# First top-k selections of six tiles moved into the joint query's loop, and index conversions on ScalarE

## The chip, the cores and the metric

The kernel runs on one core of a Trainium2 chip. The core has a matrix engine (TensorE, PE in the profile, with its weight loads as PEld), a vector engine (VectorE, DVE), an activation engine (ScalarE, ACT), a general engine (GpSimd, POOL) and an engine that only issues DMAs here (SyncE, SP). ScalarE and GpSimd issue DMAs too, in line with their other work. Each engine runs its instructions in a fixed order and waits on semaphores for the others.

The metric is the device time of one launch in microseconds, lower is better; the time before is the median of three runs.

## The reference

The kernel computes one layer of a hybrid decoder for 1024 prompt tokens and 8 x 8 sample tokens: a retention and an RWKV-7 mixer, a PEER expert layer, and a gated per-layer embedding. The change lies in the PEER part:

```python
q = (xb @ wq).reshape(PEER_BLOCK, PEER_HEADS, 2, PEER_DKEY // 2)
s = jnp.einsum('phcd,hcnd->phcn', q, keys).astype(jnp.float32)
sv, si = lax.top_k(s, PEER_TOPK)
cand = sv[:, :, 0, :, None] + sv[:, :, 1, None, :]
cv, ci = lax.top_k(cand.reshape(PEER_BLOCK, PEER_HEADS, PEER_TOPK * PEER_TOPK), PEER_TOPK)
e = (jnp.take_along_axis(si[:, :, 0], ci // PEER_TOPK, axis=-1) * PEER_NKEYS
     + jnp.take_along_axis(si[:, :, 1], ci % PEER_TOPK, axis=-1))
gsm = jax.nn.softmax(cv, axis=-1)
hval = jnp.einsum('pd,phkd->phk', xb, u_tab[e])
act = (jax.nn.gelu(hval.astype(jnp.float32), approximate=False) * gsm).astype(xb.dtype)
return jnp.einsum('phk,phkd->pd', act, v_tab[e])
```

For each token and each of 8 heads, the token's query is scored against two sets of 128 keys. The 16 best of each set are kept (the *first* selection, 16 of them per token: 8 heads x 2 halves). Their sums are candidates; the 16 best of these (the *second* selection) give 16 experts a head, 128 a token, out of 16384. Each expert is a row of `u_tab` and a row of `v_tab`, 1024 numbers each.

## The kernel before

The tokens form nine tiles, 0 to 8, of 128 tokens (tile 8, the samples, has 64). Three groups are handled in different ways in the PEER part:

- Tiles 0, 1 and 8 (`E0`) have a query of their own (`early_query`, L1172) and *gather* their expert rows: `gather` (L1117) fetches, for one expert slot of all tokens at a time, a row per token by an indirect DMA that GpSimd issues (L1127). VectorE multiplies it with the tokens and sums (L1141), once for each of 128 slots (64 for tile 8); then the same again for `v_tab`, where VectorE adds the weighted row to the accumulator (L1155).
- Tiles 2 and 3 (`G1`) share the joint query with the next group, then are gathered like the first.
- Tiles 4 to 7 (`G2`) are computed *densely*: hidden values of all 16384 experts by matmuls in 128 blocks (`hidden`, L1256), multiplied with a dense matrix of gates, and multiplied with `v_tab` (`dense`, L1285).

There is one accumulator for all gathers, so the five gathered tiles follow each other: 0, 1, 8, 2, 3.

The joint query, `c_query` (L1005), runs over 16 pairs of head and half. For each it loads the weights, splits them into a high part (ScalarE) and a low part (VectorE and GpSimd by turns, `split`, L295), multiplies both tile groups by them (three matmuls each for full precision), copies the result with ScalarE (L1023), multiplies with the keys (L1026) and copies the 128 scores a token with ScalarE into a tile `ss` (L1027). After every second pair the scores are stored to memory (`sd`, L1030).

`topk` (L1033) is run for each of these six tiles in the stage after the query. It loads the scores of all 16 pairs (L1038) and makes the first selections on VectorE: the eight largest (L1043), their places (L1044), their removal (L1045), the next eight (L1046) and their places (L1047). Then the places become floating-point numbers `sf` (L1050, L1051), candidates and their expert numbers are added up (L1058 to L1065, VectorE and GpSimd), the second selection is made (L1069 to L1073), its places are converted to `cf` (L1076) and looked up by a comparison with a row of numbers (L1082 to L1084), the softmax is formed (L1094 to L1099), and for the dense tiles the expert number is divided into its two halves (L1111 to L1115, `e12`).

`gates` (L1227) makes the dense gates of one tile: it transposes `e12` and the softmax on TensorE, copies the latter (L1234, `it`), and for every four tokens builds two one-hot matrices on VectorE (L1242), scales one of them on ScalarE (L1244), multiplies them on TensorE (L1247) and copies the product with ScalarE (L1248).

The stage after the query is written out in `build`: for each dense tile in turn its `topk` is interleaved with the `gates` of the tile before, followed by a fifth of the first 96 hidden blocks (`NPRE`); `topk` and `gather` of tile 2 stand behind the second such step, those of tile 3 behind the last. Then come the other 32 hidden blocks with the dense matmuls, and at last `ple` (L1373) with the final norm, which needs the accumulators of the gathered tiles.

The order of instructions on each engine isn't the written one. A planner in the framework simulates the program when it is built, with the written order as priority, and fixes the order on each engine by when things come ready in its simulation (`schedule_with_timeline_sim=True`). The rest of the early gathers is written behind the joint query (`run(query)`, then `run(early)`).

Of the kernel before, what the change touches and what calls it, by code (L numbers as in the profile page):

```python
# [8 lines left out]
F32 = mybir.dt.float32  # L9
# [3 lines left out]
U32 = mybir.dt.uint32  # L13
AF = mybir.ActivationFunctionType
OP = mybir.AluOpType
# [163 lines left out]
G1 = [2, 3]  # L179
# [11 lines left out]
G2 = [4, 5, 6, 7]  # L191
RSTART = 2
RRATE = 1
ERATE = 1
QB = 4
EB = 150
SIZE = {t: (64 if t == 8 else 128) for t in range(9)}


def spans(tiles):  # L200

    e = [sum(SIZE[t] for t in tiles[:i]) for i in range(len(tiles) + 1)]
    return dict(zip(tiles, e)), e[-1]
# [8 lines left out]
class K:  # L212
# [482 lines left out]
    def rw_mix(self, t):  # L695
# [282 lines left out]
        if t == 7:  # L978
            self.tail = self.ep0.tile([128, 512], F32, name="tail", tag="Wq", bufs=QB)
            nc.vector.tensor_tensor(self.tail, xf, p, op=OP.mult)  # L980
# [24 lines left out]
    def c_query(self, wp, da, parts):  # L1005

        nc, I = self.nc, self.I
        for hc in range(16):
            kT = wp.tile([128, 128], F32, name="keysT")
            nc.sync.dma_start(kT, I['keysT'][:, hc])  # L1010
            raw = da.tile([128, 8, 128], F32, name="wqr", tag="uraw", bufs=UB)
            nc.sync.dma_start(raw, I['wq'][hc])
            wh = da.tile([128, 8, 128], F32R, name="wqh", tag="uh", bufs=DW)
            wl = da.tile([128, 8, 128], F32R, name="wql", tag="ul", bufs=DW)
            self.split(wh, wl, raw, "g" if hc % 2 else "v")
            if hc % 2 == 0:
                st = [wp.tile([128, len(tiles), 2, 128], F32, name=f"ss{tiles[0]}", bufs=1) for tiles, _ in parts]
            for (tiles, x), s in zip(parts, st):
                off, n = spans(tiles)
                p = self.ps("pq", "b")  # L1020
                self.mm3(p[:, :n], lambda k: wh[:, k, :], lambda k: wl[:, k, :], lambda k: x[0][:, k], lambda k: x[1][:, k], 8)
                qT = wp.tile([128, n], F32, name=f"qT{tiles[0]}", bufs=1)
                nc.scalar.activation(qT, p[:, :n], AF.Copy)  # L1023
                p = self.ps("psc", "a")
                for i, t in enumerate(tiles):
                    nc.tensor.matmul(p[:SIZE[t], i * 128:i * 128 + 128], qT[:, off[t]:off[t] + SIZE[t]], kT, start=True, stop=True)  # L1026
                nc.scalar.activation(s[:, :, hc % 2], p[:, :len(tiles) * 128].rearrange("p (t k) -> p t k", k=128), AF.Copy)  # L1027
                if hc % 2:
                    for i, t in enumerate(tiles):
                        nc.scalar.dma_start(self.sd[t][:SIZE[t], hc - 1:hc + 1], s[:SIZE[t], i])  # L1030
            yield

    def topk(self, tp, t, s=None, tags={}, ce=None):  # L1033
        nc = self.nc
        n = SIZE[t]
        if s is None:
            w = tp.tile([128, 16, 128], F32, name="s", bufs=1)
            nc.sync.dma_start(w[:n], self.sd[t][:n])  # L1038
            s = [w[:, j] for j in range(16)]
        sv = tp.tile([128, 16, 16], F32, name="sv")  # L1040
        si = tp.tile([128, 16, 16], U32, name="si")
        for hc in range(16):
            nc.vector.max(sv[:n, hc, 0:8], s[hc][:n])  # L1043
            nc.vector.max_index(si[:n, hc, 0:8], sv[:n, hc, 0:8], s[hc][:n])  # L1044
            nc.vector.match_replace(s[hc][:n], sv[:n, hc, 0:8], s[hc][:n], -3.0e38)  # L1045
            nc.vector.max(sv[:n, hc, 8:16], s[hc][:n])  # L1046
            nc.vector.max_index(si[:n, hc, 8:16], sv[:n, hc, 8:16], s[hc][:n])  # L1047
            yield
        sf = tp.tile([128, 8, 2, 16], F32, name="sf")
        nc.vector.tensor_copy(sf[:n].rearrange("p h c k -> p (h c) k"), si[:n])  # L1050
        nc.vector.tensor_scalar(sf[:n, :, 0], sf[:n, :, 0], 128.0, None, op0=OP.mult)  # L1051
        svv = sv.rearrange("p (h c) k -> p h c k", c=2)
        cand, eid = ce or [tp.tile([128, 8, 50], F32, name=n) for n in ("cand", "eid")]
        for src, dst, eng in ((svv, cand, nc.vector), (sf, eid, nc.gpsimd)):
# [12 lines left out]
        ci = tp.tile([128, 8, 16], U32, name="ci")  # L1067
# [5 lines left out]
            nc.vector.max_index(ci[:n, h, 8:16], cv[:n, h, 8:16], cand[:n, h])  # L1073
            yield
        cf = tp.tile([128, 128], F32, name="cf")
        nc.vector.tensor_copy(cf[:n], ci[:n].rearrange("p h k -> p (h k)"))  # L1076
        ef = tp.tile([128, 128], F32, name="ef")
        io = self.c("iota")[:n, None, :50].to_broadcast([n, 16, 50])
        for h in range(8):
# [21 lines left out]
        if t == 8:  # L1101
            ei = tp.tile([128, 128], I32, name="ei", tag="ex")
            nc.vector.tensor_copy(ei[:n], ef[:n])
            for k in range(2):
                nc.scalar.dma_start(self.eid[t][64 * k:64 * k + 64], ei[:64, 64 * k:64 * k + 64])
                nc.scalar.dma_start(self.gsm[t][64 * k:64 * k + 64], gsm[:64, 64 * k:64 * k + 64])
        elif t not in G2:
            nc.vector.tensor_copy(self.eid[t][:n], ef[:n])
        else:
            ei = tp.tile([128, 128], I32, name="ei", tag="ex")  # L1110
            nc.vector.tensor_copy(ei[:n], ef[:n])  # L1111
            e1 = tp.tile([128, 2, 128], I32, name="e1")
            nc.vector.tensor_scalar(e1[:n, 0], ei[:n], 7, None, op0=OP.logical_shift_right)
            nc.vector.tensor_scalar(e1[:n, 1], ei[:n], 127, None, op0=OP.bitwise_and)
            nc.vector.tensor_copy(self.e12[t][:n], e1[:n])  # L1115

    def gather(self, gp, t, rows=("grow",), parts=1, acc=None):  # L1117

# [53 lines left out]
    def early_query(self, wp, t, wtag, wbufs, stags):  # L1172
# [31 lines left out]
        for j in range(2):  # L1204
            s.append(wp.tile([128, 8, 128], F32, name="es", tag=stags[j], bufs=QB if stags[j] == "Wq" else 1))
            nc.sync.dma_start(s[j][:n], self.sd[t][:n, 8 * j:8 * j + 8])
        yield
        ce = wp.tile([128, 2, 8, 50], F32, name="ce", tag="Wq", bufs=QB)
        yield from self.topk(wp, t, [s[j // 8][:, j % 8] for j in range(16)], dict(eq=dict(tag="xT")), (ce[:, 0], ce[:, 1]))
# [17 lines left out]
    def gates(self, wp, t):  # L1227
        nc = self.nc
        n, o = SIZE[t], self.off[t]
        p = self.ps("pit", "i").rearrange("p (a b) -> p a b", a=4)  # L1230
        for j, src in enumerate((self.e12[t][:n, 0], self.e12[t][:n, 1], self.gsm[t][:n])):
            nc.tensor.transpose(p[:, j, :n], src, self.c("ident")[:n, :n])
        it = wp.tile([128, 128], F32, name="it", bufs=2)
        nc.vector.tensor_copy(it[:, :n], p[:, 2, :n])  # L1234
        io = self.c("iota")[:, None, :].to_broadcast([128, 4, 128])
        for s in range(0, n, 64):
            last = (o + s) // 64 == self.ntok // 64 - 1
            st = self.stage[(o + s) // 64 % 2].tile([128, 128, 64], F32, name="wst", bufs=1)
            for b in range(0, 64, 4):
                oh = [wp.tile([128, 4, 128], F32, name=f"oh{j}", bufs=2) for j in range(2)]  # L1240
                for j in range(2):
                    nc.vector.tensor_tensor(oh[j], io, p[:, j, s + b:s + b + 4, None].to_broadcast([128, 4, 128]), op=OP.is_equal)  # L1242
                for j in range(4):
                    nc.scalar.activation(oh[0][:, j], oh[0][:, j], AF.Copy, scale=it[:, s + b + j:s + b + j + 1])  # L1244
                pw = self.ps("pwt", "w").rearrange("p (a b) -> p a b", a=4)
                for j in range(4):
                    nc.tensor.matmul(pw[:, j, :], oh[1][:, j, :], oh[0][:, j, :], start=True, stop=True)  # L1247
                nc.scalar.activation(st[:, :, b:b + 4].rearrange("p i t -> p t i"), pw, AF.Copy)  # L1248
                yield
            if last:  # L1250
                self.wl = st
                return
            for q in range(0, 128, WQ):
                nc.scalar.dma_start(self.wd[(o + s) // 64, :, q:q + WQ], st[:, q:q + WQ])
# [167 lines left out]
    def build(self):  # L1422
# [3 lines left out]
        with self.es:  # L1426
            self.setup()
            em, ee, eg, et, ew, ex, ep, e0, e1, e2 = (ExitStack() for _ in range(10))
# [26 lines left out]
            for _ in a:  # L1455
                for _ in range(IE):
# [3 lines left out]
            em.close()  # L1460
            cq = sb("cq", ew, bufs=2, side="right")
            parts = [G1, G2]
            self.layout(cq, [(f"ss{g[0]}", [128, len(g), 2, 128], F32, 1) for g in parts] +
                        [(f"qT{g[0]}", [128, spans(g)[1]], F32, 1) for g in parts])
            cn = sb("cn", ew, side="right")
            c1 = sb("cx1", ew, side="right")
# [2 lines left out]
            x = self.rows_of(cx, G2)  # L1469
            da = sb("dna", eg, bufs=2)  # L1470
            self.layout(da, [("uh", [128, 8, 128], F32R, DW), ("ul", [128, 8, 128], F32R, DW), ("uraw", [128, 8, 128], F32, UB)])
            tp = sb("tk", et)
            self.e12 = {}
            n3 = spans(G2[:-1])[1]
            query = self.c_query(cq, da, [(G1, x1), (G2, x)])
# [78 lines left out]
```

## Time and profile before

| what | us |
| --- | --- |
| median of 3 runs | 3917.6 (3916.54 to 3927.6) |
| profiled execution, its own time | 3925.23 |
| its span in the trace | 3923.2 |
| PE busy | 3364.1 (86%) |
| DVE busy | 3004.0 (77%) |
| POOL busy | 2342.8 (60%) |
| ACT busy | 1225.6 (31%) |

The stages that matter here, read from where their lines begin and end: the joint query from about 1811 to 2000 (in full swing from 1841), selections, gates and the first 96 hidden blocks from 2000 to 2803, the dense stage to 3745, and the end to 3923. The gathers run beside all of them, on VectorE and GpSimd, from 546 to 3781.

How to read it: busy time is the union of an engine's instructions. Matmuls are pipelined, so their busy times overlap and a stretch in which TensorE is busy isn't one in which it is at its peak; the distance between starts tells what a matmul costs. In rows of groups the columns are line, engine, operation, output and inputs with shapes, count, then busy time in us and the mean duration of one in ns, then the idle time ahead of them and what ended it. In rows of waits they are what waited and for what, total us, number of times and the longest. In rows of the timeline the first column is the start in us from the beginning of the span and the second the length.

### The profile page before, as it was taken

To read this page: it belongs to the slowest core of one execution; us is meant where nothing else is said; L and a number is where in the kernel's file an instruction comes from. 1 tells how busy PE (TensorE), PEld (TensorE's weight loads), DVE (VectorE), ACT (ScalarE), POOL (GpSimd) and SP (SyncE) were. 2 spreads that over 40 slices of the span, in tenths; PEclk is the share of its full clock that TensorE was granted. 3 is DMA by queue.
4 is the path that set the end of the run, shared out by engine and by line. 5 is a ranking of instruction groups with operands and counts; after the bars stand their busy time and mean duration, and the time that the engine had idled before them with its cause. 6 is when DMAs were issued, how large, how long until landed. Compare 5 with 4: busy or idle time off the path is not lost. (4 is left out here: it accounts for less than half of the span.)

```text
span 3923.2 us, 52738 instructions
## 1 busy us (share of the span) xinstructions
PE 3364.1 (86%) x17749; PEld 2766.9 (71%) x17749; DVE 3004.0 (77%) x5892; ACT 1225.6 (31%) x2247; POOL 2342.8 (60%) x2051
## 2 busy tenths in 40 slices
PE   8789995777869868875998899998799989899969
PEld 7688994545747756754887777787688767677757
DVE  4454487877896798876579999998877877888765
ACT  4232221111111111211322445678523333333322
POOL 5263175554364465554577778885588778887720
PEclk9799995667877658776999999999799999999989
DMA  7266558899778878888997788888999999999952
GB/s 256 68 226 207 169 198 276 273 303 307 226 243 278 297 257 273 294 300 311 321 350 259 241 289 291 326 313 327 335 342 344 333 354 357 370 367 348 327 177 72
DMA packets 465096, 1098.81 MB, mean 280 GB/s; under 512 B 74491, under 2 KB 183289, under 8 KB 459386
## 3 DMA queue, kind: packets, MB, share of 16 engines
q0 software_dynamic: 165888, 604.05, 43.9%
q1 hardware_dynamic: 237502, 389.07, 30.4%
q10 hardware_dynamic: 61436, 102.33, 7.0%
q8 instruction: 141, 2.31, 0.2%
q14 instruction: 129, 1.06, 0.1%
HBM read 992.98 MB, written 102.24 MB: 279 GB/s over the span
## 5 line engine op out<-in xcount | busy, mean ns | idle before, releaser
L1127 POOL DMA_INDIRECT grow<-in_pv,eid x576 | 573.5, 996 | 536.7 <-DVE gacc L1155 342.6
L1127 POOL DMA_INDIRECT grow<-in_pu,eid x576 | 573.9, 996 | 452.3 <-DVE grow L1141 277.8
L1155 DVE SCALAR_TENSOR_TENSOR gacc<-grow,ac,gacc 128x1024 f32<-128x1024 f32 x571 | 731.9, 1282 | 73.3 <-DMA grow<-in_pv,eid 68.8
L1141 DVE SCALAR_TENSOR_TENSOR grow<-grow,gacc 128x1024 f32<-128x1024 f32 x576 | 691.5, 1212 | 121.4 <-DMA grow<-in_pu,eid 100.7
L1300 PE MATMUL py<-ah,vl 128*128 128x512 f32 x1024 | 405.9, 402 | 31.7 <-POOL vl L301 31.4
L1300 PE MATMUL py<-ah,vh 128*128 128x512 f32 x1024 | 409.2, 400 | 18.2 <-ACT vh L297 18.1
L328 PE MATMUL ph<-cx,ul 128*128 128x512 f32 x1024 | 407.1, 398 | 9.2 <-POOL ul L301 9.2
L326 PE MATMUL ph<-cx,uh 128*128 128x512 f32 x1024 | 408.7, 399 | 7.0 <-ACT uh L297 5.3
L327 PE MATMUL ph<-cx,uh 128*128 128x512 f32 x1024 | 407.4, 398 | 0.0
L1300 PE MATMUL py<-al,vh 128*128 128x512 f32 x1024 | 405.1, 396 | 0.0
L301 POOL TENSOR_TENSOR vl<-vraw,vh 128x640 fp32r<-128x640 f32 (+2 forms) x224 | 325.6, 1459 | 42.7 <-ACT vh L297 36.7
L301 POOL TENSOR_TENSOR ul<-uraw,uh 128x1024 fp32r<-128x1024 f32 x128 | 307.9, 2406 | 35.2 <-ACT uh L297 32.8
L297 ACT ACTIVATE vh<-vraw 128x640 fp32r<-128x640 f32 (+2 forms) x224 | 154.8, 693 | 373.6 <-PE py L1300 165.5
L1300 PEld LDWEIGHTS py<-ah,vl 128*128 128x128 f32 x1024 | 193.3, 189 | 95.0 <-POOL vl L301 52.8
L1300 PEld LDWEIGHTS py<-ah,vh 128*128 128x128 f32 x1024 | 194.4, 190 | 77.1 <-ACT vh L297 36.5
L1304 DVE TENSOR_TENSOR yT<-yT,py 128x512 f32<-128x512 f32 x216 | 147.4, 684 | 121.7 <-PE py L1300 121.4
L328 PEld LDWEIGHTS ph<-cx,ul 128*128 128x128 f32 x1024 | 196.3, 192 | 51.4 <-POOL ul L301 10.9
L326 PEld LDWEIGHTS ph<-cx,uh 128*128 128x128 f32 x1024 | 196.1, 191 | 48.8 <-ACT uh L297 6.5
L327 PEld LDWEIGHTS ph<-cx,uh 128*128 128x128 f32 x1024 | 196.2, 192 | 40.3
L1300 PEld LDWEIGHTS py<-al,vh 128*128 128x128 f32 x1024 | 193.8, 189 | 43.1
L1247 PE MATMUL pwt<-oh,oh 128*128 128x128 f32 x1024 | 162.0, 310 | 63.2 <-ACT oh L1244 53.8
L1247 PEld LDWEIGHTS pwt<-oh,oh 128*128 128x128 f32 x1024 | 149.7, 213 | 84.7 <-ACT oh L1244 74.0
(401 smaller groups left out, 7815.1 us busy)
## 6 DMA issues: line engine op xcount, KB each, us to landing
uraw<-in_puT SPq DMA_DIRECT2D x128, 512.0 KB, 5.0
vraw<-in_pvd SPq DMA_DIRECT2D x152, 320.0 KB, 5.9
cw<-in_w_out SPq DMA_DIRECT2D x128, 256.0 KB, 5.5
wd<-wst ACTq DMA_DIRECT2D x28, 1024.0 KB, 15.4
wt<-wd SPq DMA_DIRECT2D x64, 448.0 KB, 7.5
wraw<-in_w_ret SPq DMA_DIRECT2D x48, 512.0 KB, 5.0
ewq<-in_wq SPq DMA_DIRECT2D x48, 512.0 KB, 5.5
gd<-geh ACTq DMA_DIRECT2D x96, 256.0 KB, 4.9
```

The lines of the kernel that those rows point to most:

```text
L297: nc.scalar.activation(hi, src, AF.Copy)
L301: nc.gpsimd.tensor_tensor(lo, src, hi.bitcast(F32), op=OP.subtract)
L326: mm(out, lh(k), rh(k), start=first and k == 0, stop=False)
L327: mm(out, lh(k), rl(k), start=False, stop=False)
L328: mm(out, ll(k), rh(k), start=False, stop=last and k == nk - 1)
L1127: nc.gpsimd.indirect_dma_start(out=g, out_offset=None, in_=src, in_offset=bass.IndirectOffsetOnAxis(ap=self.eid[t][:, j:j + 1], axis=0))
L1141: nc.vector.scalar_tensor_tensor(g[:, c], g[:, c], 1.0, x[:, c], op0=OP.mult, op1=OP.mult, accum_out=hv[:, i, j:j + 1])
L1155: nc.vector.scalar_tensor_tensor(y[:, c], g[:, c], ac[:, j:j + 1], y[:, c], op0=OP.mult, op1=OP.add)
L1247: nc.tensor.matmul(pw[:, j, :], oh[1][:, j, :], oh[0][:, j, :], start=True, stop=True)
L1300: nc.tensor.matmul(p, lh[:, b, :], rh, start=b == 0 and j == 0, stop=b == nb - 1 and j == 2)
L1304: nc.vector.tensor_tensor(yT[:, d, :], yT[:, d, :], p, op=OP.add)
```

## The change

The first selections become a function `pick`, which `c_query` calls for each tile as soon as a pair's scores are copied. The scores no longer go through memory for these tiles: the `ss` tiles hold one pair instead of two and exist three times (`SB`), and the chosen values and places stay in two tiles per token tile, `self.found`. All low parts of the query's weights are split by GpSimd. In `topk`, tiles 2 to 7 start from `self.found`; the conversions of places to `sf` and `cf`, that of the expert halves to `e12`, and the copy `it` in `gates` are made by ScalarE. The early tiles keep the old way.

```diff
+SB = 3
@@ c_query
-            self.split(wh, wl, raw, "g" if hc % 2 else "v")
-            if hc % 2 == 0:
-                st = [wp.tile([128, len(tiles), 2, 128], F32, name=f"ss{tiles[0]}", bufs=1) for tiles, _ in parts]
-            for (tiles, x), s in zip(parts, st):
+            self.split(wh, wl, raw, "g")
+            for tiles, x in parts:
                 off, n = spans(tiles)
+                s = wp.tile([128, len(tiles), 128], F32, name=f"ss{tiles[0]}", bufs=SB)
...
-                nc.scalar.activation(s[:, :, hc % 2], p[:, :len(tiles) * 128].rearrange("p (t k) -> p t k", k=128), AF.Copy)
-                if hc % 2:
-                    for i, t in enumerate(tiles):
-                        nc.scalar.dma_start(self.sd[t][:SIZE[t], hc - 1:hc + 1], s[:SIZE[t], i])
+                nc.scalar.activation(s, p[:, :len(tiles) * 128].rearrange("p (t k) -> p t k", k=128), AF.Copy)
+                for i, t in enumerate(tiles):
+                    self.pick(self.found[t], hc, s[:, i], 128)
             yield
+
+    def pick(self, found, hc, s, n):
+        nc = self.nc
+        sv, si = found
+        nc.vector.max(sv[:n, hc, 0:8], s[:n])
+        nc.vector.max_index(si[:n, hc, 0:8], sv[:n, hc, 0:8], s[:n])
+        nc.vector.match_replace(s[:n], sv[:n, hc, 0:8], s[:n], -3.0e38)
+        nc.vector.max(sv[:n, hc, 8:16], s[:n])
+        nc.vector.max_index(si[:n, hc, 8:16], sv[:n, hc, 8:16], s[:n])
@@ topk
         if s is None:
-            w = tp.tile([128, 16, 128], F32, name="s", bufs=1)
-            nc.sync.dma_start(w[:n], self.sd[t][:n])
-            s = [w[:, j] for j in range(16)]
...
+            sv, si = self.found[t]
+        else:
+            sv = tp.tile([128, 16, 16], F32, name="sv")
+            si = tp.tile([128, 16, 16], U32, name="si")
+            for hc in range(16):
+                self.pick((sv, si), hc, s[hc], n)
+                yield
         sf = tp.tile([128, 8, 2, 16], F32, name="sf")
-        nc.vector.tensor_copy(sf[:n].rearrange("p h c k -> p (h c) k"), si[:n])
-        nc.vector.tensor_scalar(sf[:n, :, 0], sf[:n, :, 0], 128.0, None, op0=OP.mult)
+        if t in G1 + G2:
+            sr = si[:n].rearrange("p (h c) k -> p h c k", c=2)
+            for c in range(2):
+                nc.scalar.activation(sf[:n, :, c], sr[:, :, c], AF.Copy, scale=(128.0, 1.0)[c])
+        else:
...
-        nc.vector.tensor_copy(cf[:n], ci[:n].rearrange("p h k -> p (h k)"))
+        if t in G1 + G2:
+            nc.scalar.activation(cf[:n], ci[:n].rearrange("p h k -> p (h k)"), AF.Copy)
+        else:
...
-            nc.vector.tensor_copy(self.e12[t][:n], e1[:n])
+            nc.scalar.activation(self.e12[t][:n], e1[:n], AF.Copy)
@@ gates
-        nc.vector.tensor_copy(it[:, :n], p[:, 2, :n])
+        nc.scalar.activation(it[:, :n], p[:, 2, :n], AF.Copy)
@@ build
-            self.layout(cq, [(f"ss{g[0]}", [128, len(g), 2, 128], F32, 1) for g in parts] +
+            self.layout(cq, [(f"ss{g[0]}", [128, len(g), 128], F32, SB) for g in parts] +
...
+            self.found = {t: (tp.tile([128, 16, 16], F32, name=f"sv{t}"), tp.tile([128, 16, 16], U32, name=f"si{t}")) for t in G1 + G2}
```

More of the change, by code (lines that the diff above doesn't have):

```diff
@@ L1036, in topk @@
         if s is None:
-            w = tp.tile([128, 16, 128], F32, name="s", bufs=1)
-            nc.sync.dma_start(w[:n], self.sd[t][:n])
-            s = [w[:, j] for j in range(16)]
[L1040 to L1048, printed above, removed]
-        sf = tp.tile([128, 8, 2, 16], F32, name="sf")
-        nc.vector.tensor_copy(sf[:n].rearrange("p h c k -> p (h c) k"), si[:n])
-        nc.vector.tensor_scalar(sf[:n, :, 0], sf[:n, :, 0], 128.0, None, op0=OP.mult)
+            sv, si = self.found[t]
[5 more added lines that the diff above has]
+                yield
+        sf = tp.tile([128, 8, 2, 16], F32, name="sf")
+        if t in G1 + G2:
[3 more added lines that the diff above has]
+        else:
+            nc.vector.tensor_copy(sf[:n].rearrange("p h c k -> p (h c) k"), si[:n])
+            nc.vector.tensor_scalar(sf[:n, :, 0], sf[:n, :, 0], 128.0, None, op0=OP.mult)
         svv = sv.rearrange("p (h c) k -> p h c k", c=2)
@@ L1075, in topk @@
         cf = tp.tile([128, 128], F32, name="cf")
-        nc.vector.tensor_copy(cf[:n], ci[:n].rearrange("p h k -> p (h k)"))
+        if t in G1 + G2:
+            nc.scalar.activation(cf[:n], ci[:n].rearrange("p h k -> p (h k)"), AF.Copy)
+        else:
+            nc.vector.tensor_copy(cf[:n], ci[:n].rearrange("p h k -> p (h k)"))
         ef = tp.tile([128, 128], F32, name="ef")
```

## The prediction, made before the changed kernel ran

> **What bounds the kernel now.** I read the profile by stages, because busy shares over 3.9 ms mix stages with different limits. First the busy time of each engine in stretches of the span, chosen by where the query's, the gates' and the dense matmuls begin and end. The columns are the stretch, its length, then for each engine its busy us and its number of instructions, then the granted clock, the DMA share and GB/s.
>
> ```profile
> core 0: us, PE busy (x) PEld busy (x) DVE busy (x) ACT busy (x) POOL busy (x), PEclk, DMA share, GB/s
> 1850.00:2000.00 150.00, 147.42 (x895) 130.44 (x895) 90.34 (x112) 46.82 (x80) 88.96 (x77) 0.99 0.94 336
> 2000.00:2050.00 50.00, 50.00 (x219) 41.35 (x218) 39.29 (x164) 14.88 (x18) 34.26 (x26) 0.99 0.93 322
> 2050.00:2350.00 300.00, 273.85 (x1216) 224.02 (x1215) 299.93 (x1003) 119.39 (x195) 216.33 (x152) 0.95 0.78 265
> 2350.00:2600.00 250.00, 227.10 (x1123) 187.92 (x1122) 242.03 (x554) 153.94 (x289) 206.32 (x152) 0.97 0.85 298
> 2600.00:2700.00 100.00, 99.72 (x554) 86.55 (x552) 81.95 (x136) 78.89 (x169) 72.34 (x53) 1.00 0.95 361
> 2700.00:2803.00 103.00, 59.83 (x305) 53.37 (x304) 92.92 (x148) 81.82 (x194) 41.14 (x41) 0.74 0.87 316
> 2803.00:3745.00 942.00, 899.23 (x3770) 705.60 (x3770) 748.78 (x1091) 325.09 (x524) 752.48 (x628) 0.99 0.98 348
> ...
> 3780.00:3923.20 143.20, 133.66 (x618) 104.60 (x616) 76.34 (x113) 41.88 (x76) 13.02 (x34) 0.99 0.22 73
> ```
>
> The reader is to see three things. In the query loop (1850 to 2000) TensorE is full and VectorE idles 150 - 90.3 = 59.7 us. In the selection stage VectorE is full: 299.93 of 300 us from 2050 to 2350. And the stage ends with 103 us in which TensorE works 59.8 us at a clock of 0.74. What that tail waits for is told by the waits of PE, its last hidden block (the Gelu behind it) and the gates' own lines:
>
> ```profile
> PE pwt L1247 <- ACT oh L1244: 35.2, 27, 5.2
> 2700.17 0.59 ACT L1267 ACTIVATE ph<-ph 128x512 f32<-128x512 f32 x1
> L1234 DVE COPY it<-pit x4: 271/278/292, 2195.8 to 2713.7; 128x128 f32<-128x128 f32 x4
> 2690.41 1.05 PE L1247 MATMUL pwt<-oh,oh 128*128 128x128 f32 x8
> 2105.52 0.39 PE L326 MATMUL ph<-cx,uh 128*128 128x512 f32 x1
> 2105.75 0.39 PE L327 MATMUL ph<-cx,uh 128*128 128x512 f32 x1
> ```
>
> The hidden blocks, filler for TensorE, run out at 2700; the gates of the last tile begin only at 2714 and run alone to 2803, at ScalarE's pace. The first tile's gates begin at 2196, some 190 us into the stage. TensorE itself needs less: 96 hidden blocks x 24 matmuls x 0.23 us (the distance of the two L326/L327 rows) = 530 us, and 1024 gate matmuls x 1.05/8 us = 134 us, so 664 of the stage's 803 us. The stage is thus set by VectorE's queue, and TensorE leaves at most 139 us to win.
>
> The other long chain is the row gather, whose five tiles follow one another on VectorE. Its instructions alone (tile grow), VectorE and GpSimd busy, and its last instructions:
>
> ```profile
> 1850.00:2000.00 150.00, 83.78 (x106) 65.70 (x67) 0.99 0.94 336
> 2000.00:2350.00 350.00, 104.15 (x110) 89.36 (x85) 0.96 0.80 273
> 2350.00:2803.00 453.00, 176.49 (x275) 148.13 (x146) 0.93 0.88 316
> 2803.00:3745.00 942.00, 452.74 (x490) 342.04 (x360) 0.99 0.98 348
> 3778.20 2.60 DVE L1155 SCALAR_TENSOR_TENSOR gacc<-grow,ac,gacc 128x1024 f32<-128x1024 f32 x2
> ```
>
> It ends at 3780.8, 36 us after the dense matmuls, and the last stage takes 143 us from there. So two chains end close together, and a gain must reach both.
>
> **The change, part by part.** First the moved selections, 96 (16 halves of 6 tiles) of each of these, and their distances in the timeline, where each find and replace has a load of its values ahead:
>
> ```profile
> L1047 DVE FIND_INDEX8 si<-sv,s 128x8 uint32<-128x128 f32 x96 | 26.4, 281 | 0.0
> L1044 DVE FIND_INDEX8 si<-sv,s 128x8 uint32<-128x128 f32 x96 | 26.2, 282 | 0.0
> L1045 DVE MATCH_REPLACE8 s<-sv,s 128x128 f32<-128x128 f32 x96 | 25.8, 273 | 0.0
> L1046 DVE MAX8 sv<-s 128x8 f32<-128x128 f32 x96 | 24.0, 277 | 0.0
> L1043 DVE MAX8 sv<-s 128x8 f32<-128x128 f32 x96 | 21.3, 275 | 0.0
> 2018.19 1.25 DVE L1043 MAX8 sv<-s 128x8 f32<-128x128 f32 x6
> 2022.47 0.07 DVE L1045 MATCH_VALUE_LOAD s<-sv,s 128x8 f32 x1
> 2022.53 0.28 DVE L1045 MATCH_REPLACE8 s<-sv,s 128x128 f32<-128x128 f32 x1
> 2022.72 0.08 DVE L1044 MATCH_VALUE_LOAD si<-sv,s 128x8 f32 x1
> ```
>
> By the busy columns they take 123.7 us, and 3 x 96 loads of 0.07 us another 20, 144 in all; but neighbours overlap: a MAX8 starts every 0.2 us (1.25 / 6), a load with its replace or find every 0.26 us. One selection is 2 x 0.2 + 3 x 0.26 = 1.18 us, 96 are **114 us**; this value I take, with 144 as the upper end (an order in which each waits for the one before). They leave the full selection stage and enter the query loop. A head of that loop takes TensorE 150/16 = 9.4 us or a little more; six selections are 7.1 us, so VectorE keeps up if they go first; program order puts them ahead of the gather steps still to come. The scores' ring of 3 lets VectorE lag about 28 us before ScalarE's copy and then the score matmuls wait.
>
> Second, the weight splits of the loop and ScalarE's part:
>
> ```profile
> L299 DVE TENSOR_TENSOR wql<-wqr,wqh 128x1024 fp32r<-128x1024 f32 x8 | 9.8, 1221 | 9.4 <-ACT wqh L297 6.0 <-PE ewo L602 3.3
> L301 POOL TENSOR_TENSOR wql<-wqr,wqh 128x1024 fp32r<-128x1024 f32 x8 | 19.1, 2383 | 3.5 <-ACT wqh L297 3.4
>   DMA sd<-ss: 22.0, 5
> ```
>
> Eight splits leave VectorE, at 1.22 us each (six of them, 7.3 us, in the counted stretch), and cost GpSimd 8 x 2.38 = 19 us; GpSimd is busy 89 of 150 us there, and four split buffers run ahead of TensorE, so I take 0, with 19 us if a split stands behind a gather issue whose buffer VectorE hasn't freed. The 48 stores of scores and the six loads go, with 22 us in which ScalarE waited for stores; TensorE was full beside them, so 0.
>
> So the loop's VectorE work is 90.3 - 7.3 + 114 = 197 us in 150: 47 us of gather are pushed out. For TensorE I take 0, with bounds of 0 and +47, the case in which nothing is pushed out.
>
> Third, the conversions that ScalarE takes over, and what ScalarE pays for a 128x128 activation:
>
> ```profile
> L1050 DVE CAST sf<-si 128x256 f32<-128x256 uint32 x6 | 2.5, 420 | 0.0
> L1051 DVE TENSOR_SCALAR sf<-sf 128x128 f32<-128x128 f32 x6 | 6.7, 1114 | 0.0
> L1076 DVE CAST cf<-ci 128x128 f32<-128x128 uint32 x6 | 9.5, 1588 | 0.1
> L1115 DVE CAST e<-e 128x256 f32<-128x256 int32 x4 | 2.6, 651 | 0.0
> L1076 DVE CAST cf<-ci x9: 205/227/4003, 486.7 to 2555.0; 128x128 f32<-128x128 uint32 x8, 64x128 f32<-64x128 uint32 x1
> L1095 ACT ACTIVATE ex<-ex x9: 303/310/313, 487.3 to 2568.9; 128x128 f32<-128x128 f32 x8, 64x128 f32<-64x128 f32 x1
>   DVE ex L1094: 28.2, 6
> ```
>
> VectorE loses 2.5 + 6.7 + 9.5 + 2.6 + 1.1 (four copies L1234) = **22.4 us**; the L1076 row shows that most is stalls (0.2 us at best, 4.0 at worst). ScalarE gains 6 x 3 x 0.31 + 4 x about 0.42 + 4 x 0.31 = 8.5 us. It is idle 181 of 300 and 96 of 250 us, so 0. Ten of the new ones (six positions, four expert halves) wait for a VectorE result with splits and gate scalings queued behind on ScalarE. The trace has the like: six waits of the softmax's Exp, 28.2 us, 4.7 each. Ten would be 47 us of ScalarE's idle time; TensorE has buffered work beside it. I take 0, with +10 as the end.
>
> One thing could make the selections dearer in the loop: beside them GpSimd now does twice as many splits. The rows show no such price in the selection stage, where GpSimd was busy 216 of 300 us: no mean of L1043 to L1047 is over 282 ns, while that of L1076 is 1588 against 205 at best. The Trainium skill ("SBUF — State Buffer", Who interferes with whom) says that a VectorE instruction with at most one SBUF input, outside the two-port modes, does not contend with GpSimd, and that casts can; the selections have one input each, and the trace agrees on both. If they did block behind the eight added splits, the loop would lose up to 19 us, and the forecast below would be 3874.
>
> **The sum.** VectorE's relief in the selection stage is 114 + 22.4 - 47 = 89 us. For the path I count from TensorE: if the gates come earlier by that much, the tail's 305 matmuls (at most 305 x 0.131 = 40 us at full pace) run among or just behind the hidden blocks, which I leave ending at 2700. The stage ends at 2740 instead of 2803: **-63 us**; ends are 0 (the gates stay last) and -89 (VectorE's relief shows whole), and TensorE's need of 664 us lies behind that. The dense stage I leave at 942 us, since TensorE is busy 899 of it, and the last stage likewise.
>
> The gather must follow. VectorE's work from 2000 to 2803 was 756 us (the sum of five rows), 281 of it gather, so 475 other; less 114 and 22 leaves 339. In 740 us there is room for 401 us of gather, and 281 + 47 = 328 are needed to enter the dense stage where it did. So the gather can shift by the 63 us too. Against the profiled execution's 3925.2 us (span 3923.2) the forecast is 3862. That execution stood 7.6 us above the median of 3917.6, so I predict **3855 us**.
>
> **The rivals.** *The gather becomes the bound* (slower). Its rows wait in an order fixed at build time. If it keeps the old pace in the selection stage, it does 281 x 740/803 = 259 us there and enters the dense stage 47 + 22 = 69 us of work behind. With the dense pace unchanged, 69 + 15 = 84 us are left when the dense matmuls end at 3682. At 0.6 us of work per us (between the dense stage's 453/942 = 0.48 and full) that takes 140 us: end of gather 3822, plus 143 gives 3965 of span, some 3960 by the median. It decides from a last gather instruction about 12 us later than 3780.8. For it: 47 us are surely pushed out. Against: the room of 401 us.
>
> *The gain goes elsewhere* (no change): the dense stage starts earlier but the gather ends at 3780 as before, and the last stage waits: about 3917.
>
> *The stage packs better* (more gain): gates and hidden blocks fill TensorE, the stage ends near 2690, and the gather uses its room: -110 us, 3805. For it speaks TensorE's need of 664 us; against, GpSimd's 216 of 300 us, through which every hidden block passes.
>
> *The change doesn't do what it says*: the planner keeps gather rows first and the selections slip behind the loop, or the loop stretches by up to 47 us, less what then need not be caught up. Only the conversions' 22 us remain: about 3900.
>
> **How the numbers follow.** Forecast 0.48, packs better 0.17, gather as the bound 0.17, no change 0.13, not as said 0.05 (about faster). About 0.3%, 12 us, is what a measurement of this kernel can tell from no change. So faster 0.70, same 0.13, slower 0.17. The range runs from 3805, the better packing, to 3945, inside the slower rival, leaving about 1 in 10 on either side; most of it is the unknown between 0 and -89 in the stage and the gather's place.
>
> **What would show it.** In the changed profile: selections between about 1845 and 2010 and VectorE over 9 tenths there, the loop's TensorE still full; the first gates before 2120; the last gate matmul near 2740 and no stretch at a clock of 0.74; dense matmuls ending near 3680; the last gather row before 3740. If the loop's matmuls wait for scores or weights, if the first gates still begin near 2190, or if the gather ends after 3780, the forecast is wrong at that step.

## The result, and the profile after

| | before | changed |
| --- | --- | --- |
| median of 5 runs, us | 3916.5 (3914.5 to 3927.6) | 3884.3 (3873.8 to 3890.5) |
| ratio to before | | 0.991 (0.9889 to 0.9931) |
| span of the profiled execution | 3923.2 | 3874.8 |
| last score matmul of the query loop | 1998.9 | 1990.8 |
| first gates matmul | 2199 | 2139 |
| last gates matmul | 2797 | 2744 |
| dense matmuls | 2804 to 3747 | 2752 to 3701 |
| last gather instruction | 3781 | 3751 |

The change makes the kernel some 32 us faster by the medians. The two spans differ by 48 us, of which 6.5 us lie ahead of the query loop: its first score matmul starts at 1839.0 instead of 1845.5. Those 6.5 us can't be put down to the change, because four kernels of this study whose code is the same up to the selections (the kernel before and three of the experiments) start it anywhere from 1833.4 to 1845.5, and all traces from 1832.6 to 1847.9. So single traces are compared below by stages, not by spans. From the last score matmul to the first dense one the kernel before took 805 us, the changed one 761: **43 us less** (a second trace of the changed kernel has 766, 39 less). The dense matmuls took 944 and 949 us, and what follows them 176 and 174.

The busy time of each engine in the stretches that were shown of before (same columns; the last two follow the earlier end of the dense matmuls):

```profile
1850.00:2000.00 150.00, 148.16 (x904) 131.62 (x903) 149.21 (x731) 48.48 (x80) 77.81 (x60) 1.00 0.69 224
2000.00:2050.00 50.00, 50.00 (x222) 41.42 (x221) 48.65 (x240) 16.79 (x24) 42.49 (x37) 1.00 0.92 321
2050.00:2350.00 300.00, 272.85 (x1224) 218.63 (x1224) 265.46 (x500) 130.88 (x226) 258.60 (x187) 0.98 0.88 299
2350.00:2600.00 250.00, 237.60 (x1243) 202.40 (x1242) 219.57 (x394) 181.35 (x370) 201.20 (x148) 0.98 0.90 321
2600.00:2700.00 100.00, 95.49 (x532) 82.72 (x531) 72.88 (x122) 80.58 (x178) 58.22 (x44) 1.00 0.90 336
2700.00:2803.00 103.00, 81.27 (x365) 67.82 (x364) 81.07 (x117) 55.49 (x118) 64.24 (x54) 0.85 0.93 335
2803.00:3701.00 898.00, 854.54 (x3567) 673.06 (x3566) 711.88 (x1048) 308.22 (x499) 713.36 (x599) 0.98 0.98 347
3701.00:3874.80 173.80, 139.98 (x640) 109.09 (x639) 104.24 (x139) 44.92 (x82) 30.37 (x51) 0.92 0.39 130
```

VectorE's 59.7 idle us of the query loop are filled (149.21 of 150), and TensorE beside it is as full as before. In the selection stage VectorE is no longer full: 265.46 instead of 299.93 us of the 300 from 2050 to 2350. What it does in the loop, by groups of one shape (columns as in the groups shown of before):

```profile
L1039 DVE FIND_INDEX8 si<-sv,ss 128x8 uint32<-128x128 f32 x96 | 26.8, 297 | 0.0
L1036 DVE FIND_INDEX8 si<-sv,ss 128x8 uint32<-128x128 f32 x96 | 26.6, 295 | 0.0
L1037 DVE MATCH_REPLACE8 ss<-sv,ss 128x128 f32<-128x128 f32 x96 | 25.9, 287 | 0.0
L1038 DVE MAX8 sv<-ss 128x8 f32<-128x128 f32 x96 | 23.5, 290 | 0.0
L1035 DVE MAX8 sv<-ss 128x8 f32<-128x128 f32 x96 | 22.9, 289 | 1.3 <-ACT ss L1027 1.3
```

And its gather alone (tile grow; VectorE and GpSimd busy):

```profile
1850.00:2000.00 150.00, 53.52 (x59) 41.66 (x45) 1.00 0.69 224
2000.00:2350.00 350.00, 143.74 (x168) 121.28 (x116) 0.98 0.88 302
2350.00:2752.00 402.00, 153.19 (x252) 127.29 (x129) 0.96 0.90 328
2752.00:3701.00 949.00, 454.67 (x491) 343.03 (x363) 0.98 0.98 346
```

In the loop's 150 us, 731 - 59 = 672 instructions aren't gather: 84 selections of eight instructions, in 149.2 - 53.5 = 95.7 us, 1.14 us each. The gather has 53.5 us there instead of 83.8, and makes it up after the loop: 143.7 us from 2000 to 2350 instead of 104.2.

The conversions on ScalarE, by groups of one shape, and the wait of the gates' matmuls for ScalarE:

```profile
L1056 ACT ACTIVATE sf<-si 128x128 f32<-128x128 uint32 x12 | 3.3, 303 | 14.8 <-DVE si L1039 11.1 <-POOL eid L1073 3.2 <-ACT geh L1278 0.4
...
L1085 ACT ACTIVATE cf<-ci 128x128 f32<-128x128 uint32 x6 | 1.9, 311 | 3.2 <-DVE eq L1093 3.0 <-DVE ci L1081 0.2
...
L1126 ACT ACTIVATE e<-e 128x256 f32<-128x256 int32 x4 | 1.6, 411 | 4.9 <-DVE e L1125 4.9
L1245 ACT ACTIVATE it<-pit 128x128 f32<-128x128 f32 x4 | 1.2, 304 | 0.0
```

```profile
PE pwt L1258 <- ACT oh L1255: 32.5, 28, 4.8
```

They cost ScalarE 8.0 us, and 22.9 us of its idle time ended with one of them. The place conversions that averaged 1588 ns on VectorE average 311 here, beside a GpSimd that is busy 258.6 of 300 us. The Trainium skill ("SBUF — State Buffer", Who interferes with whom) gives ScalarE a read and a write port of its own and lets VectorE share a pair with GpSimd; these rows agree with it.

**Where the gain stopped.** The expert halves of the four dense tiles, which the gates wait for, come earlier by 59, 71, 86 and 87 us (starts in the trace: 2183.3, 2297.2, 2482.4 and 2568.4 before; 2124.7, 2226.6, 2396.8 and 2481.4 after). The gates don't follow. From a line's own view (shortest, median and longest in ns, first and last start), the expert halves before and after, then the copy `it` with which the gates of a tile begin:

```profile
L1115 DVE CAST e<-e x4: 270/282/1772, 2183.3 to 2568.4; 128x256 f32<-128x256 int32 x4
L1126 ACT ACTIVATE e<-e x4: 399/414/418, 2124.7 to 2481.4; 128x256 f32<-128x256 int32 x4
```

```profile
L1245 ACT ACTIVATE it<-pit x4: 273/309/324, 2130.3 to 2654.5; 128x128 f32<-128x128 f32 x4
```

In the changed kernel 6 us lie between the expert halves and `it` for the first tile, 173 for the last; before, 12.5 and 145. ScalarE's timeline shows where the gates got stuck. Each group of four tokens ends with a copy of its product into a stage tile (L1248 before, L1259 after). Before, then after:

```profile
2276.50 1.09 ACT L1248 ACTIVATE wst<-pwt 128x512 f32<-128x512 f32 x1
...
2363.34 1.02 ACT L1159 ACTIVATE gy<-gacc 128x1024 f32<-128x1024 f32 x1 [2.91 <-DVE gacc L1155]
2364.39 0.33 ACTq L1160 DMA_DIRECT2D yd<-gy  x1
...
2367.22 1.94 ACT L1248 ACTIVATE wst<-pwt 128x512 f32<-128x512 f32 x2 [0.56 <-ACT geh L1267]
```

```profile
2210.94 1.12 ACT L1259 ACTIVATE wst<-pwt 128x512 f32<-128x512 f32 x1 [0.40 <-PE pwt L1258]
...
2326.11 1.03 ACT L1170 ACTIVATE gy<-gacc 128x1024 f32<-128x1024 f32 x1 [2.67 <-DVE gacc L1166]
...
2327.53 0.33 ACTq L1171 DMA_DIRECT2D yd<-gy  x1
...
2329.27 1.12 ACT L1259 ACTIVATE wst<-pwt 128x512 f32<-128x512 f32 x1
```

In both kernels the first half of the first dense tile (16 groups) is followed by a hole in the gates, and the second half starts right behind the line that stores the accumulator of tile 8, the last early gather: 91 us of hole before, 118 after. The remaining 112 groups then take 431 and 416 us, 3.8 and 3.7 us each. So most of the 52 us by which the last gates came earlier (2744 instead of 2797) is the earlier start of the second half, 38 us; a quicker pace behind it gave the other 14. That start hung on the end of the early gather, which came only 37 us earlier: the loop's selections push the gather out first, and VectorE's relief gives it back afterwards. The second half goes to the second of two stage tiles. It lies in a pool (`keep`) whose memory overlaps that of the early gathers' buffers, while the first half's tile lies in a pool of the gates (`gw`):

```python
self.stage = (gw, kp)
...
st = self.stage[(o + s) // 64 % 2].tile([128, 128, 64], F32, name="wst", bufs=1)
```

### The profile page after: what moved, and what is told of

It is laid out like the page before. It is cut to its first block, busy times and chain, and to the rows that moved or that the text cites. A ratio compares the mean times of both kernels' runs of the same rounds, so it can differ in the third digit from the quotient of the medians.

```text
span 3874.8 us, 52635 instructions
## 1 busy us (share of the span) xinstructions
PE 3343.9 (86%) x17749; PEld 2756.1 (71%) x17749; DVE 2968.1 (77%) x5858; ACT 1228.2 (32%) x2273; POOL 2361.0 (61%) x2059
## 4 chain that ended last, share of the span: by engine, by line
PE 38%; DVE 19%; DMA 13%; POOL 10%; issue 9%; ACT 2%; ACTq 0%; POOLq 0%; SPq 0%; DVEq 0%
PE py L1311 13%; POOL grow L1138 5%; DVE grow L1152 4%; PE ph L329 3%; PE ph L327 3%; PE ph L328 3%; DMA grow<-in_pu,eid 3%; DVE gacc L1166 3%; DMA grow<-in_pv,eid 3%; POOL vl L302 2%; PE pwt L1258 2%; PE epq L1206 2%; PE ewo L612 1%; DMA ft<-fd 1%; DVE si L1036 1%
## 5 line engine op out<-in xcount | busy, mean ns | idle before, releaser
L298 ACT ACTIVATE uh<-uraw 128x1024 fp32r<-128x1024 f32 x128 | 135.4, 1058 | 268.4 <-DMA uraw<-in_puT 133.5
L1253 DVE TENSOR_TENSOR oh<-csta,pit 128x512 f32<-128x512 f32 x256 | 161.9, 680 | 45.1 <-PE pwt L1258 42.7
```

The source lines that it names most:

```text
L298: nc.scalar.activation(hi, src, AF.Copy)
```

## The experiments

Every ratio below is to runs of the kernel before that were made together with it. The first four kernels take the change apart and test the wait. Their theories: VectorE's relief by the selections carries the gain; ScalarE's part of it is small; the moved splits are free; and the hole is either a wait on memory at run time or a place in the planned order.

**Selections alone.** The changed kernel, with the conversions, the copy `it` and the splits as before:

```diff
-            self.split(wh, wl, raw, "g")
+            self.split(wh, wl, raw, "g" if hc % 2 else "v")
...
-            nc.scalar.activation(self.e12[t][:n], e1[:n], AF.Copy)
+            nc.vector.tensor_copy(self.e12[t][:n], e1[:n])
...
-        nc.scalar.activation(it[:, :n], p[:, 2, :n], AF.Copy)
+        nc.vector.tensor_copy(it[:, :n], p[:, 2, :n])
```

> The moved selections alone (conversions and the weight splits as before). Theory A, the relief of VectorE by 114 us carries the gain: about 25 us under the kernel before (ratio near 0.9935), most of the changed kernel's 32. Theory B, the conversions' stalls were what held the lookups: within 10 us of before. Either way the last expert halves of the dense tiles come about 70 us earlier than 2568 under A, under 20 us earlier under B.

Measured: 0.9937 of before (0.9913 to 0.996), 25 us, as theory A had it. The last expert halves came at 2488, 81 us earlier. The second half of the first gates started at 2353.

**Conversions alone.** The kernel before, with `sf`, `cf`, `e12` and `it` made by ScalarE:

```diff
-        nc.vector.tensor_copy(cf[:n], ci[:n].rearrange("p h k -> p (h k)"))
+        if t in G1 + G2:
+            nc.scalar.activation(cf[:n], ci[:n].rearrange("p h k -> p (h k)"), AF.Copy)
+        else:
...
-            nc.vector.tensor_copy(self.e12[t][:n], e1[:n])
+            nc.scalar.activation(self.e12[t][:n], e1[:n], AF.Copy)
```

> The conversions on ScalarE alone, selections where they were. Theory A: within 10 us of before, since 22 us of VectorE are a fifth of the relief. Theory B: 20 us or more under before.

Measured: 0.9921 (0.989 to 0.9952), 31 us. That they are a small part fell: within the intervals, 22 us of VectorE's time bring as much as 114 us of selections do. In this trace the last early gather ended at 2326 instead of 2363. The two parts gain in different places (copies of the gates' products, us in the trace):

| kernel | second half starts | last copy ends | between |
| --- | --- | --- | --- |
| before | 2367 | 2798 | 431 |
| selections alone | 2353 | 2760 | 407 |
| conversions alone | 2331 | 2765 | 434 |
| changed | 2329 | 2746 | 416 |

The conversions bring the second half forward by 36 us, as far as the early gather's end, and nothing behind it. The selections bring it forward by only 14 us; their other 24 us come from a quicker pace of the remaining gates. One trace of each stands behind this.

**Splits by turns.** The changed kernel, with only the splits of the query's weights as before (the first two lines of the diff above).

> The changed kernel with the query's weight splits by turns on VectorE and GpSimd as before. If GpSimd's 8 added splits (19 us) cost nothing: within 8 us of the changed kernel (about 3884), with 10 us of VectorE back in the loop. If they held the gather's issues in the loop: 10 us or more under it.

Measured: 0.9928 (0.9906 to 0.9951) where the changed kernel has 0.991. The intervals overlap, so whether GpSimd's splits help isn't settled; they do no harm that shows. In this trace the second half began at 2355 instead of 2329; the query loop itself began 9 us later.

**Memory order.** The changed kernel, with the early gathers' buffers laid out so that the second stage tile overlaps only an unused ring (`Wq`):

```diff
-            self.layout(ep0, [("V", [128, D], F32, 2), ("W", [128, D], F32, 1), ("xy", [128, D], F32, 1), ("Wq", [128, D], F32, QB), ("xT", [128, D], F32, 1)])
+            self.layout(ep0, [("Wq", [128, D], F32, QB), ("V", [128, D], F32, 2), ("W", [128, D], F32, 1), ("xy", [128, D], F32, 1), ("xT", [128, D], F32, 1)])
```

> The changed kernel with the early pool's tiles laid out so that the second gate tile lies on buffers that the last early gather doesn't use; the order on every engine is the same. Theory W, the gates' second half waits at run time for that memory: it starts near 2215 instead of 2329, and the time is 20 to 35 us under the changed kernel. Theory O, the planned order alone puts it there: no difference, it starts at about 2329 again.

Measured: 0.9876 (0.9845 to 0.9906); the interval overlaps that of the changed kernel (0.991). ScalarE's timeline:

```profile
2211.66 1.12 ACT L1259 ACTIVATE wst<-pwt 128x512 f32<-128x512 f32 x1 [0.40 <-PE pwt L1258]
...
2327.33 1.03 ACT L1170 ACTIVATE gy<-gacc 128x1024 f32<-128x1024 f32 x1 [2.90 <-DVE gacc L1166]
...
2330.30 1.11 ACT L1259 ACTIVATE wst<-pwt 128x512 f32<-128x512 f32 x1
```

The copy stands where it stood, though the bytes it writes aren't those of the gathers any more. In the changed kernel two waits on semaphores stand right ahead of it, in the view of its line:

```profile
L1259 ACTq EVENT_SEMAPHORE  x2: 38/38/38, 2328.8 to 2328.9; - x2
```

In this kernel the same view (2190 to 2400) has none: the copy no longer waits for that memory. The instructions stand in the same order as the changed kernel's (but for neighbours that differ between two traces of the changed kernel as well). So theory O holds: the hole is in the planned order, in which the copy stands on ScalarE behind the store of the early accumulator, whatever it would have to wait for. Why the planner puts it there even in this layout isn't shown.

The next kernels take the wait away, in the changed kernel and in the one before, and try the next candidate beside it: the 48 lookups of places (L1093 to L1095), which use one tile `eq` by turns on VectorE and GpSimd.

**Stage tiles of the gates' own pool.** The changed kernel; the first three halves use the first stage tile, and the second comes into use later:

```diff
-            st = self.stage[(o + s) // 64 % 2].tile([128, 128, 64], F32, name="wst", bufs=1)
+            st = self.stage[(o + s) // 64].tile([128, 128, 64], F32, name="wst", bufs=1)
...
-                self.stage = (gw, kp)
+                self.stage = (gw, gw, gw, kp, gw, kp, gw, kp)
```

> The changed kernel with the first three halves of the gates written to the first stage tile, one after another, instead of by turns to the two: the second half then waits for a store of some 20 us and not for the early gather's end. Theory G, that wait binds the stage: the second half starts before 2260 (2329 in the changed kernel), the last gate matmul comes 15 to 30 us earlier than 2745, and the time is 15 to 30 us under the changed kernel. Theory P, TensorE's filler of hidden blocks binds (they end at 2706 either way): the gates come earlier but the time stays within 8 us.

Measured: **0.9786 (0.9763 to 0.9809), 3835.6 us**, 81 us under before: the fastest kernel of the study. ScalarE's timeline and the selection stage by engine:

```profile
2217.43 1.13 ACT L1259 ACTIVATE wst<-pwt 128x512 f32<-128x512 f32 x1 [0.40 <-PE pwt L1258]
...
2239.88 1.95 ACT L1259 ACTIVATE wst<-pwt 128x512 f32<-128x512 f32 x2 [3.75 <-DMA wd<-wst]
```

```profile
2050.00:2350.00 300.00, 277.31 (x1331) 227.96 (x1331) 282.96 (x563) 165.26 (x313) 251.89 (x181) 0.98 0.87 299
2350.00:2600.00 250.00, 238.68 (x1253) 201.29 (x1253) 215.10 (x388) 185.31 (x378) 199.69 (x145) 0.99 0.90 324
2600.00:2700.00 100.00, 99.35 (x553) 86.01 (x552) 70.89 (x119) 79.87 (x169) 60.17 (x44) 1.00 0.92 339
2700.00:2803.00 103.00, 96.86 (x416) 79.15 (x415) 69.25 (x108) 33.71 (x51) 84.49 (x66) 0.97 0.95 338
```

The hole is 22 us, the time until the first half is stored. The last gates matmul ends at 2703, 42 us earlier, among the hidden blocks; the Gelu that was the stage's last in the changed kernel (2706) is at 2709 here. Two more hidden blocks run before the dense matmuls begin at 2728, and none of these stretches has a clock under 0.97. Against the changed kernel measured beside it (3879.3, below) the edit brings 44 us, more than the 15 to 30 of theory G. The wait was thus what held the change's gain back.

**The same edit in the kernel before.** Its two lines are L1238 and L1504 there.

> The same edit in the kernel before. Theory G: 15 to 35 us under before, a good part of what the change brings. Theory V, VectorE's full queue alone binds there: within 10 us of before, since VectorE is full until 2350 and gates earlier push the gather later.

Measured: 0.9924 (0.9899 to 0.9948), 30 us. The wait cost the kernel before too. With it gone in both, the change is worth (0.9924 - 0.9786) x 3916.6 = **54 us**, where it is worth 32 to 38 us with it.

**Two lookup tiles.** The changed kernel; the expert halves' tile takes `sf`'s place to make room:

```diff
-            eq = tp.tile([128, 16, 50], F32, name="eq", **tags.get("eq", {}))
+            eq = tp.tile([128, 16, 50], F32, name="eq", **tags.get("eq", dict(bufs=2)))
...
-            e1 = tp.tile([128, 2, 128], I32, name="e1")
+            e1 = tp.tile([128, 2, 128], I32, name="e1", tag="sf")
```

> The changed kernel with two tiles for the lookup's comparison instead of one (48 lookups of VectorE, GpSimd, VectorE follow one another at about 10.6 us each). If that chain binds: expert halves of the last tile 50 us or more before 2481 and the time 10 us or more under the changed kernel. Theories G and P: the halves come earlier, the time stays within 8 us.

**The changed kernel again**, beside the last three:

> The changed kernel once more, beside the others of this call: about 3884, 32 us under before, with its profile's query loop beginning within 12 us of 1839.

Measured: 0.9876 (0.9851 to 0.99) with two lookup tiles, 0.9902 (0.9875 to 0.9928) for the changed kernel; the intervals overlap. The last expert halves came at 2403 instead of 2480, 77 us earlier, and the median moved by 9 us. The first half of the gates was done earlier, but the second still began behind the early gather's store, at 2344 instead of 2328: the lookups aren't what the stage waits for, as long as the hole stands.

The last three kernels ask what the parts are worth without the wait.

**Stage tiles and two lookup tiles**, both edits in the changed kernel:

> The changed kernel with both edits, the stage tiles and two lookup tiles. With the gates no longer held by the early gather's end, an earlier expert half can count: 3825 to 3836, that is 0 to 10 us under the stage edit alone (3836). If hidden blocks on TensorE bind there (they ended at 2709 with either), no difference.

**Conversions alone with the stage edit**, and **selections alone with the stage edit**:

> The kernel before with the conversions on ScalarE and the stage tiles. If the conversions' gain of some 25 us came through the early gather's earlier end (2326 for 2363), most of it is gone here: within 10 us of the kernel before with the stage tiles (3887). If it came through VectorE's queue in the whole stage: about 3862.

> The kernel before with the moved selections and the stage tiles. With the wait gone the relief of VectorE shows more than the 24 us it brought with the wait: 3845 to 3855, some 35 us under the kernel before with the stage tiles (3887). If hidden blocks bind instead: 3870 or more.

| with the stage edit | ratio (interval) | dense matmuls end | last gather row ends | span |
| --- | --- | --- | --- | --- |
| nothing else | 0.9924 (0.9899 to 0.9948) | 3713 | 3782 | 3885.9 |
| conversions | 0.9934 (0.991 to 0.9958) | 3708 | 3781 | 3881.5 |
| selections | 0.9851 (0.9827 to 0.9875) | 3648 | 3803 | 3845.3 |
| the whole change | 0.9786 (0.9763 to 0.9809) | 3657 | 3780 | 3833.0 |
| the change, two lookup tiles | 0.9854 (0.9825 to 0.9884) | 3652 | 3819 | 3858.2 |

The conversions alone bring nothing that shows once the wait is gone, so their 31 us came through the early gather's end. The selections bring 0.9924 - 0.9851, 29 us, about what was expected. The last row is a miss: more relief made the kernel slower than the changed kernel with the stage edit alone. The table's columns say why. In the first, second and fourth rows the span ends 173 to 176 us behind the dense matmuls, as it does in all other traces of the study (172 to 176). In the other two it ends 198 and 206 us behind them, but 42 and 39 us behind the last gather row. So the time is set by the later of two: dense end plus some 175, or gather end plus some 40. The end of VectorE's timeline, two lookup tiles first, then the stage edit alone:

```profile
3815.25 3.93 DVE L1166 SCALAR_TENSOR_TENSOR gacc<-grow,ac,gacc 128x1024 f32<-128x1024 f32 x3
3826.29 1.22 DVE L1402 TENSOR_TENSOR ph<-ph,py 128x1024 f32<-128x1024 f32 x1 [7.11 <-DMA py<-yd]
...
3853.47 1.41 DVE L1430 SCALAR_TENSOR_TENSOR fin<-ph,frs,row_norm_final 128x512 f32<-128x512 f32 x2 [2.19 <-POOL frs L293]
```

```profile
3778.66 1.28 DVE L1166 SCALAR_TENSOR_TENSOR gacc<-grow,ac,gacc 128x1024 f32<-128x1024 f32 x1
...
3792.42 1.23 DVE L1402 TENSOR_TENSOR ph<-ph,py 128x1024 f32<-128x1024 f32 x1 [1.88 <-DMA ph<-hd]
...
3828.20 1.42 DVE L1430 SCALAR_TENSOR_TENSOR fin<-ph,frs,row_norm_final 128x512 f32<-128x512 f32 x2 [2.18 <-POOL frs L293]
```

In the first, VectorE idles 7.11 us until the accumulator just stored is read back (L1402), and only one tile's last steps follow: the gather is the bound. In the second the last tile has its accumulator in time. The gather's VectorE time from 2000 to 2350 in both, in the same order, tells what two lookup tiles did:

```profile
2000.00:2350.00 350.00, 117.02 (x145) 104.08 (x95) 0.97 0.82 275
```

```profile
2000.00:2350.00 350.00, 139.35 (x161) 113.16 (x108) 0.99 0.87 301
```

The gather had 22 us less of VectorE beside work that could start earlier; the early gather ended at 2422 instead of 2353, and the gather's end stayed 39 us late. Likewise the conversions are worth the step from 0.9851 to 0.9786, (0.9851 - 0.9786) x 3916 = 25 us, only with the selections: their 22 us of VectorE bring the gather's end from 3803 to 3780, below the other bound. That explanation rests on these ends; no kernel was run that moves the gather alone.

## Why the prediction was right, and where it was not

The median came out 29 us above the forecast of 3855, inside the range and faster as forecast, with about half of the forecast gain. That it fell inside is owed to the width of the range, which left the stage anywhere from 0 to -89, more than to the path by which the gain was to come: that path had an order in it that the prediction didn't see. By its steps:

- **The query loop.** Right: 1.14 us a selection against 1.18; 83.8 - 53.5 = 30 us of gather pushed out up to 2000, and the 10 selections left after 2000 (two ran before 1850) another 11, together 41 against 47; TensorE full (148.16 of 150). Selections were to lie between 1845 and 2010; they lie between 1840 and 2024. VectorE's wait for scores in the loop was 1.3 us.
- **Splits on GpSimd.** No cost showed, as forecast. Selections beside them averaged 287 to 297 ns in the rows above, where they had 273 to 282: at 15 ns on 480 of them at most 7 us, not the 19 of a block. Even this isn't the splits: in the second trace of the changed kernel the same rows have 270 to 280 ns, and with the splits by turns 280 to 289.
- **Conversions.** The sizes were right (8.0 us of ScalarE against 8.5), and the waits they add came to 22.9 us of idle ScalarE, without an effect that shows. Their effect on the path was not what the prediction had: it put them into one sum of VectorE's relief. Alone, they act through the gather's place.
- **The relief of 89 us.** Its size came out: the last tile's expert halves came 87 us earlier. In part this is luck, since alone the selections, with the splits by turns, brought them forward by 81 us (the same sum gives 114 - 54 = 60) and the conversions by 39 (22). The step that failed is the next one, "if the gates come earlier by that much, the tail's 305 matmuls ... run among or just behind the hidden blocks". It took VectorE's queue as the gates' only releaser. The first gates matmul came 59 us earlier (2139, where "before 2120" was asked), the second half of the first tile only 38 us, because ScalarE's planned order held it behind the early gather's store. The term of -63 measured **-43**, and with that hole gone (the stage edit in the changed kernel) -73. The hole was visible before: the gates of the first tile have a hole of 91 us in ScalarE's timeline that ends 3 us behind the early gather's store.
- **The ends.** The last gates matmul ended at 2744 (2740 forecast) and the last hidden block at 2706 (2700). The numbers nearly agree although the reason doesn't: the last gates were late not because they follow the hidden blocks but because of the hole. The stretch at a low clock was to go; from 2700 to 2803 it is at 0.85 instead of 0.74, and in the kernel without the wait at 0.97.
- **Dense and last stage unchanged.** Right in the changed kernel (949 against 944 us, 174 against 176), the end at 3701 where 3680 was asked. In the four kernels that end their gates earliest the dense matmuls took 929 to 933 us, in all others 941 to 955. Part of this is that 100 or 101 of the 128 hidden blocks ran ahead of the first dense matmul there, and 99 in all others: at 24 x 0.23 = 5.5 us a block, 6 to 11 us have only moved from one stage to the other; the rest stays open. So 99 blocks stood in the stage before too, not 96, and TensorE's need was some 680 us rather than 664.
- **The gather follows.** It ended at 3751, 11 us later than asked and 30 earlier than before, 85 us before it would decide (3701 + 175 - 40 - 3751).
- **The slower rival** had its mechanism right and its price wrong. "The last stage takes 143 us from there" (the gather's end) was read from one trace in which the dense end decided; from a gather that decides it takes some 40. Its point of decision, "about 12 us later", was read off the same wrong price: in the kernel before the gather had 3747 + 175 - 40 - 3781 = 101 us to spare. The rival showed itself in the two kernels above, 23 and 31 us behind what their dense end allowed.
- **"Packs better"** came nearest in the kernel with the stage edit: TensorE is busy 99.35 of the 100 us from 2600 on, the gates end among the hidden blocks, and it is 81 us under before where the rival had 110. Its dense matmuls begin at 2728, not near 2690.

## What to carry to other kernels

Before a relief is put into a sum, look in the timeline of each engine behind it for a hole that ends right behind something unrelated: an order fixed when the program is built can hold work behind an instruction whose result and memory it doesn't need at run time, and much of the relief then counts only as far as it moves that instruction. When two chains end near each other, the distance from one's end to the kernel's end is its price only in a trace where that chain is the last; take several traces and look which distance stays the same. Work that becomes ready earlier can take its engine from what ran there before: two lookup tiles brought the expert halves forward and made the best kernel some 25 us slower.

## What the runs showed of the hardware that was not expected

Single traces of four kernels with the same code ahead begin the query loop's score matmuls anywhere from 1833.4 to 1845.5, and the runs of one kernel spread by 11 to 40 us, so a difference under some 15 us between two spans tells nothing. Longer runs tend to have the lower granted clock (of 21 runs of the kernel before, the shortest has 3898.2 us at 0.881, the longest 3938.1 at 0.869); which of the two follows from the other isn't shown. In two traces of the changed kernel, with the same instructions, the means of the moved selections differ by some 6%, 287 to 297 ns in one and 270 to 280 in the other. Two kernels with the same order of instructions and different addresses (the memory order above) had 0.9876 and, in other runs, 0.991 and 0.9902; the intervals overlap, so an effect of the addresses is neither shown nor excluded.
